# Reordering ScalarE around the query projections, the stores around the norms, and moving paired gate products to VectorE in a two-layer encoder kernel

## The chip, the cores and the metric

The kernel runs on one core of a Trainium2 chip. The metric is the device time of one execution in microseconds (us); the time shown for the kernel before is the median of three runs.

## The reference

256 tokens of width 1024 pass two layers. Each layer has an attention mixer and an expert mixer, each followed by a layer norm:

```python
for i in range(2):
    m = _mla_mixer(...) if i == 0 else _dsa_mixer(...)
    x = _layernorm(DN_ALPHA * x + m, ln_gain[i, 0], ln_bias[i, 0])
    f = _peer(x, peer_w_q[i], peer_sub_keys[i], peer_w_down[i], peer_w_up[i])
    x = _layernorm(DN_ALPHA * x + f, ln_gain[i, 1], ln_bias[i, 1])

def _peer(x, w_q, sub_keys, w_down, w_up):
    q = (xt @ w_q).reshape(T, 8, 2, 128)
    s1, s2 = scores of both halves of q against 128 sub-keys for each head
    v1, i1 = lax.top_k(s1, 16);  v2, i2 = lax.top_k(s2, 16)
    best, pos = lax.top_k(v1 + v2 over all pairs, 16)       # for each token and head
    gate = softmax(best)                                    # 128 experts for each token
    a = x . w_down[expert];  y = sum(gelu(a) * gate * w_up[expert])
```

The expert mixer has 128 x 128 = 16384 experts.

## The kernel before

**Numbers as pairs.** Every float32 weight and activation becomes two float16 parts: `hi`, a rounded copy that ScalarE casts (line 89), and `lo`, the remainder that VectorE computes with a running sum (line 98). One product is three float16 matmuls (hi.hi, hi.lo, lo.hi), issued by `mm` (line 340). Activations are `xh` and `xl`.

**The weight stream.** All weights pass in one fixed order through the class `Stream`, in blocks of 128 x 1024. A block is loaded by SyncE's queue (line 133) into one of six `raw` buffers, cast to `hi`, reduced to `lo`, used by TensorE, and dropped; there are six `hi` and six `lo` buffers. `get` hands out the next block and first splits blocks up to three further on (`AHEAD`) and issues loads up to five beyond those. Four blocks of the query weights are loaded ahead into the arena (line 141). With `ws.share = POOLED`, every fourth block is split in another way: ScalarE scales it in place (line 164) and casts it (166), GpSimd subtracts (168), and ScalarE later sums the result (177). In the stretches with much VectorE work this takes load off VectorE.

**Order.** A scheduler that simulates the program decides the order of instructions on each engine. `tc.issue_after` forces one instruction behind another of the same engine. `chains` holds such forced orders by engine: while `chains["dve"]` is open, all that is issued through `dve(...)` keeps the program's order; `act(...)` and `pe(...)` do the same where their chain is open.

**The norms (`finish`).** The last four weight blocks of a mixer are multiplied first for token tile 0 and then for tile 1, so that norm 0 runs on VectorE and ScalarE while TensorE does tile 1. `queue` keeps the order written out by hand on each engine. `Turned` transposes a normed tile on TensorE and splits it; the first four blocks of what follows (values of the second attention, or queries of the experts) are then multiplied part by part. A part is named by two letters, activation first: `lh` is `xl` with the block's `hi`. `ws.open` queues a block's cast, `ws.close` its `lo`. The normed tiles go to DRAM (`keep`, lines 515 and 529) and come back much later.

**The queries (`peer`).** The first 512 query columns come out of `finish` in two PSUM banks; `unscale` copies them out (line 372), `turn` transposes them (1080, 1081). `queries(n)` then projects two blocks and copies the result into `qT`; `scores(g4)` multiplies four of them with the keys and copies the scores (1103) to SBUF. The choosing of experts (`choose`, lines 1106 to 1170) is VectorE work that `spend` deals out in the program's order between the blocks.

**The down projection and the gates.** 128 blocks of `w_down` follow, two for a round of the loop. Once the choice is made, each round also calls `prepare` for one or two groups of four tokens: VectorE compares (line 1241, `hot`), GpSimd multiplies half of the comparison by the gates (1243), ScalarE multiplies the other way (1247). In the next round `place` lets TensorE combine them (`G`) and ScalarE and VectorE copy the result to the arena (1260, 1262). `hot` and `gate` have two buffers each. 60 of the 64 groups come two in a round. Then follow 128 blocks of `w_up` and the next norm.

Of the kernel before, what the change touches and what calls it, by code (L numbers as in the profile page):

```python
# [15 lines left out]
ALU = mybir.AluOpType  # L16
AX = mybir.AxisListType

P = 128
# [81 lines left out]
class Stream:  # L101
# [94 lines left out]
    def open(self, queue):  # L196

        i = self.n_split
        assert i == self.n_taken
        self._high(i, lambda emit: queue("act", emit))  # L200
        self.n_split += 1
        self.n_taken += 1
        return i
# [38 lines left out]
def tile_trunk(ctx: ExitStack, tc: tile.TileContext, ins, out: bass.AP, short, shared):  # L242
    nc = tc.nc
    half = F16 if short else F32R
    unit, ranks, total_unit = (UNIT, RANKS, SUM) if short else (1.0, 1.0, 1.0)
# [31 lines left out]
    keep = [dram.tile([P, D], F32, tag=f"x{t}", name=f"x{t}") for t in range(2)]  # L277
# [3 lines left out]
    gate16 = const.tile([P, T], F16, tag="gate16", name="gate16")  # L281
# [18 lines left out]
    ws = Stream(nc, raws, rings, half, split, spare16)  # L300
# [17 lines left out]
    chains = {}  # L318
# [17 lines left out]
    def act(emit):  # L336
        return link("act", emit)
# [33 lines left out]
    def unscale(o, p, unit):  # L371
        return nc.scalar.mul(o, p, 1.0 / unit) if short else nc.scalar.copy(o, p)
# [99 lines left out]
    def finish(y4, lhs_of, n, g, b, x, spare, lead=None):  # L472

        blks = [ws.get(ahead=0) for _ in range(STAGGER)]
        queue = queue_of()
        last = None
        norms = []  # L480
        for t in range(2):
            with ExitStack() as order:
                if last is not None:
                    order.enter_context(tc.issue_after(last.ins))
                for i, blk in enumerate(blks):
                    k = n - STAGGER + i
                    last = rows(y4, lhs_of(k), blk, k == 0, k == n - 1, (t,))
            if lead is not None:
                norms.append(Norm(queue, x[t], y4[t], g, b, spare[t], spare[2 + t], spare[4]))
        if lead is None:  # L490
            if short:
                judge()

            def close():
                queue = queue_of()
                for t in range(2):
                    norm = Norm(queue, x[t], y4[t], g, b, spare[t], spare[2 + t], spare[4], shared["st"][t])
                    norm.sums()
                    norm.square()
                    norm.centre()  # L500
                    norm.scale()
                    norm.result()
                for t in range(2):
                    for h, q in enumerate((nc.sync, nc.scalar)):
                        s = slice(h * 512, (h + 1) * 512)
                        q.dma_start(out[t * P : (t + 1) * P, s], spare[t][:, s])

            return close
        n0, n1 = norms
        n0.sums()  # L510
        n0.square()
        n0.centre()
        n0.scale()
        n0.result()
        nc.sync.dma_start(keep[0], spare[0])
        queue("pe", lambda: last)
        x0, x1 = Turned(queue, 0, spare[0]), Turned(queue, 1, spare[1])
        blk = [ws.open(queue) for _ in range(3)]
        n1.sums()
        x0.high(0, 2)  # L520
        x0.high(1, 4)
        n1.square()
        x0.low(0)
        n1.centre()
        blk.append(ws.open(queue))
        n1.scale()
        x0.low(1)
        n1.result()
        nc.sync.dma_start(keep[1], spare[1])
        unit = lead(queue)  # L530

        def do(t, part, *ks):
            for k in ks:
                unit(t, part, k, ws.ready[blk[k]])

        do(0, "hh", 0, 1, 2)
        do(0, "lh", 0, 1, 2)
        do(0, "hh", 3)
        do(0, "lh", 3)
        x1.high(0, 2)  # L540
        x1.high(1, 4)
        do(1, "hh", 0, 1, 2, 3)
        ws.close(blk[0], queue)
        ws.close(blk[1], queue)
        x1.low(0)
        do(0, "hl", 0, 1)
        do(1, "lh", 0, 1)
        do(1, "hl", 0, 1)
        ws.close(blk[2], queue)
        x1.low(1)  # L550
        do(0, "hl", 2)
        do(1, "hl", 2)
        do(1, "lh", 2)
        ws.close(blk[3], queue)
        do(0, "hl", 3)
        do(1, "hl", 3)
        do(1, "lh", 3)

    def weigh_up(part, lo, hi):

# [489 lines left out]
    def peer(li):  # L1050
# [3 lines left out]
        qT, keys = ar.take(16, T), ar.take(16, NKEYS)  # L1054
        s = [ar.take(16, NKEYS) for _ in range(2)]
# [12 lines left out]
        scr = ar.ring(2, NKEYS)  # L1068
        qrow = [arena[:, middle - (2 - t) * 512 : middle - (1 - t) * 512] for t in range(2)]
        tail = s[0].rearrange("p a b -> p (a b)")  # L1070
        nc.sync.dma_start(keys, ins["keys"][li].rearrange("n p k -> p n k"))

        for t, q in enumerate(begun.pop("q")):
            unscale(qrow[t], q, unit)

        def turn():
            for t in range(2):
                p = ps(f"qwT{t}")
                for n in range(4):
                    nc.tensor.transpose(p[:, n * P : (n + 1) * P], qrow[t][:, n * P : (n + 1) * P], ident)  # L1080
                nc.scalar.copy(qT[:, 0:4, t * P : (t + 1) * P], p.rearrange("p (n t) -> p n t", t=P))

        def queries(n):
            p = ps(f"pq{n}")
            pv = p.rearrange("p (j t) -> p j t", t=T)
            first = proj(pv[:, 0, :], ws.get())
            if n == FIRST:
                with tc.issue_after(first.ins):
                    turn()
            else:  # L1090
                spend(PACE)
            proj(pv[:, 1, :], ws.get())
            if n > FIRST:
                spend(PACE)
            unscale(qT[:, n : n + 2, :], pv, unit)

        def scores(g4):
            for t in range(2):
                p = py((2 * g4 + t) % 4, f"ps{g4}{t}")
                for j in range(4):  # L1100
                    n = 4 * g4 + j
                    mm(p[:, j * P : (j + 1) * P], qT[:, n, t * P : (t + 1) * P], keys[:, n, :], True, True)
                nc.scalar.copy(s[t][:, 4 * g4 : 4 * g4 + 4, :], p.rearrange("p (j k) -> p j k", k=P))

        def top16(vals, ids, src, buf):
            dve(lambda: nc.vector.max(vals[:, 0:8], src))
# [115 lines left out]

        chains["dve"] = None
        ws.dve = dve
        queries(4)
        ws.share = POOLED
        scores(0)
        queries(6)
        scores(1)
        for g4 in range(2, 4):  # L1230
            queries(4 * g4)
            queries(4 * g4 + 2)
            scores(g4)

        onehot = {}

        def prepare(g4):
            hot = ohp.tile([P, 2, P, 4], F16, tag="V", name="hot")
            gate = ohp.tile([P, 2, 4, P], F16, tag="U", name="gate")
            four = slice(4 * g4, 4 * g4 + 4)  # L1240
            nc.vector.tensor_tensor(hot, iota4[:, None].to_broadcast([P, 2, P, 4]),  # L1241
                                    place16[:, :, None, four].to_broadcast([P, 2, P, 4]), op=ALU.is_equal)
            nc.gpsimd.tensor_tensor(gate[:, 0], hot[:, 1].rearrange("p c j -> p j c"),  # L1243
                                    gate16[:, four, None].to_broadcast([P, 4, P]), op=ALU.mult)
            for j in range(4):
                t = 4 * g4 + j
                nc.scalar.mul(gate[:, 1, j, :], hot[:, 1, :, j], rest[:, t : t + 1])  # L1247
            onehot[g4] = hot, gate
# [18 lines left out]
        for b0 in range(0, NKEYS, 2):  # L1267
            p = ps(f"d{b0}")
            pv = p.rearrange("p (j t) -> p j t", t=T)
            chosen = ready  # L1270
            for j in range(2):
                proj(pv[:, j, :], ws.get())
                ready = ready or spend(PACE)
            if b0 == 0:
                chains["pe"] = None
            t0 = 4 * groups
            if t0 < T:
                nc.scalar.activation(A[:, b0 : b0 + 2, t0:], pv[:, :, t0:], AF.Gelu, scale=1.0 / unit)
            if t0 > 0:
                nc.scalar.activation(pv[:, :, :t0], pv[:, :, :t0], AF.Gelu, scale=1.0 / unit)  # L1280
                nc.vector.tensor_tensor(A[:, b0 : b0 + 2, :t0], A[:, b0 : b0 + 2, :t0], pv[:, :, :t0], op=ALU.mult)
            while groups < prepared:
                place(groups, b0 + 2)
                groups += 1
            if chosen:
                left = max(1, (NKEYS - 4 - b0) // 2)
                want = min(64 - groups, -(-(64 - groups) // left))
                assert want <= 2
                for _ in range(want):
                    prepare(prepared)  # L1290
                    prepared += 1
        assert groups == 64, groups
        chains.pop("pe")
# [188 lines left out]
```

## Time and profile before

| | |
|---|---|
| median of 3 runs | 1723.12 us (1722.04 to 1723.86) |
| the profiled execution's own time | 1721.89 us |
| span in its profile | 1720.0 us |
| TensorE busy | 1700.1 us (99%) |
| VectorE / ScalarE / GpSimd busy | 1346.4 / 1096.4 / 393.6 us |
| moved from DRAM | 329.16 MB |

The rows are read so: a group of instructions has its line in the kernel, engine, operation, output and inputs; then shape, count, total busy time and mean duration; behind the bar's second part stands how long the engine had been idle in front of them and what ended that. A row of the timeline has start and length in us. DVE is VectorE, ACT is ScalarE, POOL is GpSimd, PE is TensorE, SP is the queue of DMAs.

### The profile page before, as it was taken

The page shows a single profiled execution, that of the slowest core. Times are in us where ns is not written, and L with a number is a line of the kernel's source. Part 1 is how long each engine was busy: PE and PEld are TensorE (multiplying, and loading weights), DVE is VectorE, ACT ScalarE, POOL GpSimd, SP SyncE. Part 2 cuts the span into 40 slices and gives each one's busy share as a digit, 9 for nine tenths or more (in the row PEclk, how much of TensorE's full clock was granted, in tenths as well). Part 3 has the DMA queues.
Part 4 walks back from the last instruction along what each step waited for, and adds up shares of the span by engine and source line. Part 5 has one row for each costly group of instructions (what it writes and reads, how often), then busy time and mean ns, then how long its engine had stood idle before and what let it go on. Part 6 is the DMA issues. An engine that isn't in the chain of part 4 may idle for free.

```text
span 1720.0 us, 33157 instructions
## 1 busy us (share of the span) xinstructions
PE 1700.1 (99%) x12495; PEld 1191.9 (69%) x12495; DVE 1346.4 (78%) x3032; ACT 1096.4 (64%) x1910; POOL 393.6 (23%) x257
## 2 busy tenths in 40 slices
PE   9999999999999999999999999999999999999998
PEld 7678888899984444444577698888999954444443
DVE  7679999989996566666688798999899966666665
ACT  7666656888875555555477656567888755554553
POOL 2011244555530000000022012454555400000000
PEclk9999999999999999999999999999999999999999
DMA  9454556655567666666565555566555576666662
GB/s 350 138 177 169 198 190 204 204 172 172 173 194 244 200 207 201 203 205 201 185 229 186 183 184 177 193 205 223 173 173 173 173 248 204 206 201 204 203 202 77
DMA packets 93483, 335.61 MB, mean 195 GB/s; under 512 B 10368, under 2 KB 11392, under 8 KB 93312
## 3 DMA queue, kind: packets, MB, share of 16 engines
q1 hardware_dynamic: 93024, 332.87, 58.6%
q8 instruction: 100, 1.64, 0.4%
q14 instruction: 71, 0.58, 0.1%
q10 hardware_dynamic: 288, 0.52, 0.1%
HBM read 329.16 MB, written 4.19 MB: 194 GB/s over the span
## 4 chain that ended last, share of the span: by engine, by line
PE 87%; DVE 5%; ACT 3%; issue 2%; DMA 1%; POOL 1%; DVEq 0%; POOLq 0%; ACTq 0%
PE y L340 40%; PE d L340 36%; PE G L340 3%; PE pq L340 2%; DVE lo L98 2%; ACT hi L89 1%; PE qw L340 1%; PE h L340 1%; PE ps L340 1%; PE qi L340 1%; PE o L340 0%; PE v L340 0%; DVE arena L997 0%; PE qn L340 0%; DMA raw<-in_down 0%
## 5 line engine op out<-in xcount | busy, mean ns | idle before, releaser
L98 DVE SCALAR_TENSOR_TENSOR lo<-raw,hi 128x1024 f16<-128x1024 f32 (+1 forms) x571 | 776.6, 1363 | 237.4 <-ACT hi L89 233.6
L89 ACT ACTIVATE hi<-raw 128x1024 f16<-128x1024 f32 (+1 forms) x571 | 594.6, 1049 | 292.2 <-PE y L340 183.4
L340 PE MATMUL d<-xh,lo 128*128 128x256 f16 x2048 | 558.3, 273 | 1.7 <-DVE lo L98 1.5
L340 PE MATMUL d<-xh,hi 128*128 128x256 f16 x2048 | 558.2, 273 | 0.0
L340 PE MATMUL d<-xl,hi 128*128 128x256 f16 x2048 | 558.2, 273 | 0.0
L340 PEld LDWEIGHTS <-hi 128*128 128x128 f16 x5016 | 488.1, 98 | 57.9 <-issue 1.3
L340 PEld LDWEIGHTS <-xh 128*128 128x128 f16 x2320 | 226.4, 98 | 270.8 <-ACT xh L89 2.4
L340 PE MATMUL y<-lo,xh 128*128 128x512 f16 x1088 | 326.3, 379 | 0.0
L340 PE MATMUL y<-hi,xh 128*128 128x512 f16 x1088 | 326.0, 379 | 0.0
L340 PE MATMUL y<-hi,xl 128*128 128x512 f16 x1088 | 325.6, 379 | 0.0
L340 PEld LDWEIGHTS <-lo 128*128 128x128 f16 x2508 | 245.5, 98 | 32.7 <-DVE lo L98 3.7
L1243 POOL TENSOR_TENSOR gate<-hot,gate 128x512 f16<-128x512 f16 x128 | 219.7, 1736 | 186.8 <-DVE hot L1241 186.8
L340 PEld LDWEIGHTS <-xl 128*128 128x128 f16 x1160 | 113.3, 98 | 138.1 <-DVE xl L98 2.5
L1247 ACT ACTIVATE gate<-hot,rest 128x128 f16<-128x128 f16 x512 | 165.8, 410 | 8.1 <-DVE hot L1241 8.1
L89 ACT ACTIVATE xh<-arena 128x512 f16<-128x512 f32 x132 | 82.5, 628 | 132.5 <-PE y L340 132.2
L98 DVE SCALAR_TENSOR_TENSOR xl<-arena,xh 128x512 f16<-128x512 f32 x134 | 91.7, 687 | 60.0 <-ACT xh L89 59.9
L168 POOL TENSOR_TENSOR lo<-raw,hi 128x1024 f16<-128x1024 f32 x26 | 58.0, 2232 | 194.8 <-ACT hi L166 155.8
L438 POOL TENSOR_TENSOR st<-st,mhalf 128x1 f32<-128x1 f32 x6 | 3.3, 554 | 414.2 <-DVE st L436 414.2
L164 ACT ACTIVATE raw<-raw 128x1024 f32<-128x1024 f32 x26 | 27.5, 1056 | 101.2 <-DMA raw<-in_down 81.3
L1165 POOL TENSOR_TENSOR arena<-arena 128x800 f32<-128x800 f16 x32 | 72.4, 2262 | 70.4 <-DVE arena L1162 62.2
L1241 DVE TENSOR_TENSOR hot<-iota,place 128x1024 f16<-128x1024 f16 x128 | 82.8, 689 | 7.0 <-PE G L340 4.6
L580 POOL TENSOR_SCALAR fit<-fit 128x2 f32<-128x2 f32 x1 | 0.2, 227 | 316.2 <-DVE junk L562 316.2
(209 smaller groups left out, 1574.6 us busy)
## 6 DMA issues: line engine op xcount, KB each, us to landing
raw<-in_down SPq DMA_DIRECT2D x256, 512.0 KB, 3.3
raw<-in_up SPq DMA_DIRECT2D x256, 512.0 KB, 4.3
raw<-in_peer_q SPq DMA_DIRECT2D x24, 512.0 KB, 4.5
raw<-in_dsa_qk SPq DMA_DIRECT2D x16, 512.0 KB, 4.8
raw<-in_mla_w_o SPq DMA_DIRECT2D x8, 512.0 KB, 5.8
arena<-in_peer_q SPq DMA_DIRECT2D x8, 512.0 KB, 6.0
raw<-in_dsa_v SPq DMA_DIRECT2D x8, 512.0 KB, 4.4
raw<-in_dsa_w_o SPq DMA_DIRECT2D x8, 512.0 KB, 3.9
```

What stands on the lines that cost most here:

```text
L89: return nc.scalar.copy(o, src) if unit == 1.0 else nc.scalar.mul(o, src, unit)
L98: return nc.vector.scalar_tensor_tensor(o, src, unit, hi, op0=ALU.mult, op1=ALU.subtract, accum_out=total)
L164: self.act(lambda: nc.scalar.mul(raw, raw, unit))
L168: nc.gpsimd.tensor_tensor(lo, raw, hi if short else hi.bitcast(F32), op=ALU.subtract)
L340: return pe(lambda: nc.tensor.matmul(o, l, r, start=start, stop=stop, skip_group_check=True))
L438: nc.gpsimd.tensor_tensor(st[:, 5:6], st[:, 4:5], mhalf, op=ALU.pow)
L580: nc.gpsimd.tensor_scalar(fit[:, 0:2], fit[:, 0:2], MOST * SMALL, None, op0=ALU.is_lt)
L1165: nc.gpsimd.tensor_tensor(o.rearrange("p k c -> p c k"), same, cell[t][:, h, :, None].to_broadcast([P, CELLS, TOPK]), op=ALU.mult)
L1241: nc.vector.tensor_tensor(hot, iota4[:, None].to_broadcast([P, 2, P, 4]), place16[:, :, None, four].to_broadcast([P, 2, P, 4]), op=ALU.is_ ...
L1243: nc.gpsimd.tensor_tensor(gate[:, 0], hot[:, 1].rearrange("p c j -> p j c"), gate16[:, four, None].to_broadcast([P, 4, P]), op=ALU.mult)
L1247: nc.scalar.mul(gate[:, 1, j, :], hot[:, 1, :, j], rest[:, t : t + 1])
```

## The change

Four parts:

1. In `finish`, the casts of the next two blocks are queued ahead of norm 0's work on ScalarE, and the `lo` of the first ahead of norm 0's work on VectorE. A part `hl` of block 0 moves forward between the `lh` parts. The store of tile 1 is issued behind the last weight load of this place.
2. In `peer`, `chains["act"]` is opened, so that ScalarE follows the program from here to the end of the queries; the keys' load is put behind a weight load.
3. The queries take blocks without splitting further ones (`get(0)`); `ws.fill` splits the next ones behind the copies of the scores.
4. `prepare` gives the gates' product (line 1243) to VectorE in rounds with two groups, to GpSimd in rounds with one.

```diff
@@ finish
+        blk = [ws.open(queue) for _ in range(2)]
+        ws.close(blk[0], queue)
         n0.sums()
         n0.square()
...
         x0, x1 = Turned(queue, 0, spare[0]), Turned(queue, 1, spare[1])
-        blk = [ws.open(queue) for _ in range(3)]
+        blk.append(ws.open(queue))
...
         n1.result()
-        nc.sync.dma_start(keep[1], spare[1])
...
         do(0, "hh", 0, 1, 2)
-        do(0, "lh", 0, 1, 2)
+        do(0, "lh", 0, 1)
+        do(0, "hl", 0)
+        do(0, "lh", 2)
...
         do(1, "hh", 0, 1, 2, 3)
-        ws.close(blk[0], queue)
         ws.close(blk[1], queue)
         x1.low(0)
-        do(0, "hl", 0, 1)
+        do(0, "hl", 1)
...
+        with tc.issue_after(ws.last):
+            nc.sync.dma_start(keep[1], spare[1])
@@ peer
-        nc.sync.dma_start(keys, ins["keys"][li].rearrange("n p k -> p n k"))
+        chains["act"] = None
+        ws.act = act
+        ws.fill(ws.n_taken + 1)
+        with tc.issue_after(ws.last):
+            nc.sync.dma_start(keys, ins["keys"][li].rearrange("n p k -> p n k"))
         for t, q in enumerate(begun.pop("q")):
-            unscale(qrow[t], q, unit)
+            act(lambda: unscale(qrow[t], q, unit))
+        ws.fill(ws.n_taken + 3)
...  (the copies in turn, queries and scores go through act(...) likewise)
         def queries(n):
-            first = proj(pv[:, 0, :], ws.get())
+            i = ws.n_taken
+            first = proj(pv[:, 0, :], ws.get(0))
...
-            proj(pv[:, 1, :], ws.get())
+            proj(pv[:, 1, :], ws.get(0))
...
+            return i + 5
...
-        queries(4)
+        upto = queries(4)
         ws.share = POOLED
         scores(0)
-        queries(6)
+        ws.fill(upto)
+        upto = queries(6)
         scores(1)
+        ws.fill(upto)
         for g4 in range(2, 4):
-            queries(4 * g4)
-            queries(4 * g4 + 2)
+            ws.fill(queries(4 * g4))
+            upto = queries(4 * g4 + 2)
             scores(g4)
+            ws.fill(upto)
+        chains.pop("act")
...
-        def prepare(g4):
+        def prepare(g4, engine):
...
-            nc.gpsimd.tensor_tensor(gate[:, 0], hot[:, 1].rearrange("p c j -> p j c"),
-                                    gate16[:, four, None].to_broadcast([P, 4, P]), op=ALU.mult)
+            engine.tensor_tensor(gate[:, 0], hot[:, 1].rearrange("p c j -> p j c"),
+                                 gate16[:, four, None].to_broadcast([P, 4, P]), op=ALU.mult)
...
-                    prepare(prepared)
+                    prepare(prepared, nc.gpsimd if want == 1 else nc.vector)
```

More of the change, by code (lines that the diff above doesn't have):

```diff
@@ L198, in open @@
         i = self.n_split
-        assert i == self.n_taken
         self._high(i, lambda emit: queue("act", emit))
@@ L1080, in turn @@
                     nc.tensor.transpose(p[:, n * P : (n + 1) * P], qrow[t][:, n * P : (n + 1) * P], ident)
-                nc.scalar.copy(qT[:, 0:4, t * P : (t + 1) * P], p.rearrange("p (n t) -> p n t", t=P))
+                act(lambda: nc.scalar.copy(qT[:, 0:4, t * P : (t + 1) * P], p.rearrange("p (n t) -> p n t", t=P)))
         def queries(n):
@@ L1091, in queries @@
                 spend(PACE)
-            proj(pv[:, 1, :], ws.get())
+            proj(pv[:, 1, :], ws.get(0))
             if n > FIRST:
                 spend(PACE)
-            unscale(qT[:, n : n + 2, :], pv, unit)
+            act(lambda: unscale(qT[:, n : n + 2, :], pv, unit))
+            return i + 5
         def scores(g4):
@@ L1102, in scores @@
                     mm(p[:, j * P : (j + 1) * P], qT[:, n, t * P : (t + 1) * P], keys[:, n, :], True, True)
-                nc.scalar.copy(s[t][:, 4 * g4 : 4 * g4 + 4, :], p.rearrange("p (j k) -> p j k", k=P))
+                act(lambda: nc.scalar.copy(s[t][:, 4 * g4 : 4 * g4 + 4, :], p.rearrange("p (j k) -> p j k", k=P)))
         def top16(vals, ids, src, buf):
```

## The prediction

> **What bounds the kernel now.** I read the page first, then TensorE's waits, then the chain of waits, then the timeline at the three places that the change touches.
>
> ```profile
> span 1720.0 us, 33157 instructions
> PE 1700.1 (99%) x12495; PEld 1191.9 (69%) x12495; DVE 1346.4 (78%) x3032; ACT 1096.4 (64%) x1910; POOL 393.6 (23%) x257
> ```
>
> TensorE is busy in 99% of the span. The change removes no matmul, so all that it can win is idle time of TensorE, 19.9 us in the whole span, start and end included. TensorE's waits, in total, times, longest:
>
> ```profile
> PE G L340 <- POOL gate L1243: 1.8, 4, 0.5
> PE d L340 <- DVE lo L98: 1.5, 2, 1.0
> PE ps L340 <- ACT arena L372: 1.4, 1, 1.4
> PE qw L340 <- DVE xl L98: 1.3, 2, 0.8
> ...
> PE qwT L1080 <- ACT arena L372: 0.7, 1, 0.7
> ```
>
> Four rows belong to the change: G 1.8, ps 1.4, qw 1.3, qwT 0.7, together 5.2 us in eight waits. A wait costs more than its idle time shows, because the end of a matmul is drawn late:
>
> ```profile
> L340 PE MATMUL d<-xh,hi 128*128 128x256 f16 x2048 | 558.2, 273 | 0.0
> 328.10 5.24 PE d L340 x48
> ```
>
> A matmul lasts 273 ns in the record, but 48 take 5.24 us, 109 ns each. So each wait hides a further 0.16 us, and eight are worth 5.2 + 1.3 = 6.5 us. That is the ceiling of this change at its own places, 0.4% of the run. By the spread of the runs before (1722.04 to 1723.86), about 0.2%, 3.4 us, can be told from no change.
>
> **The change part by part.**
>
> *Norms.* Casting two blocks ahead of norm 0 (two ScalarE casts of about 1 us, one `lo` of 1.2 us on VectorE) falls into idle time at the first norm:
>
> ```profile
> 83.05 1.15 ACT L426 ACTIVATE arena<-arena,st 128x1024 f32<-128x1024 f32 x1 [4.98 <-DVE st L421]
> 81.46 0.69 DVE L418 SCALAR_TENSOR_TENSOR arena<-arena,y 128x512 f32<-128x512 f32 x1 [1.93 <-PE y L340]
> 90.08 0.68 DVE L98 SCALAR_TENSOR_TENSOR xl<-xt,xh 128x512 f16<-128x512 f32 x1
> 90.83 0.60 PE L340 MATMUL qw<-hi,xl 128*128 128x512 f16 x2 [0.55 <-DVE xl L98]
> 957.04 1.06 ACT L164 ACTIVATE raw<-raw 128x1024 f32<-128x1024 f32 x1 [5.53 <-DMA raw<-in_peer_q]
> 958.01 1.13 ACT L426 ACTIVATE arena<-arena,st 128x1024 f32<-128x1024 f32 x1
> 956.88 0.21 DVE L421 TENSOR_SCALAR st<-st 128x1 f32<-128x1 f32 x1
> ```
>
> ScalarE waits 4.98 us and VectorE 1.93 us for TensorE there, so the early work costs nothing while raw data and ring slots are in place; without that cover, norm 0 would move by up to 1.2 us. TensorE then reaches `lh` of block 2 before `xl` is there (0.55 us). The moved `hl` of block 0 is two matmuls of 0.216 us that need no new `xl`: 0.43 us of this wait is filled. At the norm of the second attention the same wait is about 0.76 us (1.3 less 0.55). There ScalarE scaled a block of the queries (957.04, waiting for its DMA) in front of norm 0's square, which VectorE had made ready at 957.1; it started at 958.01. With the forced order that scaling belongs behind the scores, so norm 0 comes 0.9 us sooner and the wait goes whole, 0.92 us with its hidden part. Sum: -0.43 - 0.92 = -1.35 us. The norm before the second attention's values has no row among the waits: 0.
>
> *Store and keys.* SP's queue is in order:
>
> ```profile
> 92.63 1.71 SPq L529 DMA_DIRECT2D x<-arena  x1
> 94.45 12.73 SPq L133 DMA_DIRECT2D raw<-in_peer_q  x6
> 101.65 1.06 ACT L164 ACTIVATE raw<-raw 128x1024 f32<-128x1024 f32 x1 [3.05 <-DMA raw<-in_peer_q]
> 103.56 1.06 ACT L372 ACTIVATE arena<-qw 128x512 f32<-128x512 f32 x2
> ```
>
> The store of tile 1 waits for the norm's result, and six loads wait behind it until 94.45. ScalarE then stands 3.05 us for that data, and the copy of the first queries (103.56), ready about 101, comes late: TensorE's wait for it (qwT) is 0.7 us. Loads in front, and the copies in front of further casts, take this away: -0.89 us. The store is read hundreds of us later; the keys are needed by the first scores, which come behind the copies of 103.56, some 10 us after the store's turn: 0 for both. That slack is the keys' cover; without it the scores would wait.
>
> *Queries.* The wait at ps has the same kind of cause:
>
> ```profile
> 137.87 1.06 ACT L164 ACTIVATE raw<-raw 128x1024 f32<-128x1024 f32 x1 [5.71 <-DMA raw<-in_down]
> 139.78 0.58 ACT L372 ACTIVATE arena<-pq 128x512 f32<-128x512 f32 x1
> 118.83 1.07 ACT L1103 COPY arena<-ps 128x512 f32<-128x512 f32 x2
> 119.00 2.13 POOL L168 TENSOR_TENSOR lo<-raw,hi 128x1024 f16<-128x1024 f32 x1 [10.19 <-ACT hi L166]
> 126.48 1.06 PE L340 MATMUL ps<-arena 128*128 128x128 f32 x8
> ```
>
> The last query copy (139.78) stood behind a scaling that waited 5.71 us for a down block. In the new order that block's work follows the copy: -1.4 - 0.16 = -1.58 us. But the order also takes something. In the first expert mixer the block that goes through GpSimd is the first one split behind each of three scores. From the end of a query block ScalarE now copies (0.6), waits for scores (1.1), copies (1.1), scales and casts (2.0), then GpSimd takes 2.13: 6.9 us. TensorE meanwhile has 0.9 us of scores and 48 matmuls, 5.2 us, and needs the `lo` 0.2 us later: 6.3 us. Up to 0.6 us late, three times: between 0 and 1.8, I take 1.0. In the second mixer the GpSimd block is the second of its pair and has a block's 24 matmuls, 2.6 us, more: 0.3 for what I don't see (bounds 0 and 1.6, one more ps wait). VectorE's choosing starts behind the same `lo` as before, so nothing comes from there.
>
> *Gates.* At the start of each gate stage GpSimd is late for four G's: -1.8 - 4 x 0.16 = -2.44 us. The price is VectorE's time in the 29 rounds that follow, in each mixer:
>
> ```profile
> L1241 DVE TENSOR_TENSOR hot<-iota,place 128x1024 f16<-128x1024 f16 x128 | 82.8, 689 | 7.0 <-PE G L340 4.6
> 327.76 1.29 DVE L1241 TENSOR_TENSOR hot<-iota,place 128x1024 f16<-128x1024 f16 x2
> 328.97 2.08 DVE L98 SCALAR_TENSOR_TENSOR lo<-raw,hi 128x1024 f16<-128x1024 f32 x1
> 338.76 1.23 DVE L98 SCALAR_TENSOR_TENSOR lo<-raw,hi 128x1024 f16<-128x1024 f32 x1 [0.37 <-ACT hi L89]
> 328.53 3.43 POOL L1243 TENSOR_TENSOR gate<-hot,gate 128x512 f16<-128x512 f16 x2 [2.43 <-DVE hot L1241]
> ```
>
> Four rounds as windows (us; PE, PEld, DVE, ACT, POOL busy):
>
> ```profile
> 327.04:333.18 6.14, 6.14 (x67) 5.61 (x66) 5.37 (x10) 5.47 (x14) 3.43 (x2) 1.00 0.56 191
> 376.11:382.24 6.13, 6.13 (x66) 5.60 (x65) 5.60 (x10) 5.39 (x14) 3.44 (x2) 1.00 0.52 169
> 425.18:431.31 6.13, 6.13 (x67) 5.60 (x64) 5.89 (x10) 5.28 (x14) 3.44 (x2) 1.00 0.50 172
> 492.64:498.78 6.14, 6.14 (x67) 5.61 (x66) 6.12 (x10) 5.12 (x14) 3.44 (x2) 1.00 0.54 175
> ```
>
> TensorE needs 6.13 us for a round; VectorE 5.37 early and 6.12 late, since its copies of G grow. One `lo` of each round takes 2.08 us, not 1.23, beside GpSimd: without GpSimd's products VectorE gets 0.85 us back. A gate product has 512 elements. No row shows it on VectorE. The nearest is `hot`, the same operation kind, 1024 float16 elements, 0.60 us from start to start (1.29 - 0.69). `lo`, also 1024 elements, takes 1.23 (1.15 from start to start): `hot` does two elements in the time of one, so 512 at one each cost what `hot` costs, 0.60. Lower bound 0.35 (two each again); upper bound 1.15, the price of 1024 single ones. I take 0.60, and 1.20 for the pair: VectorE's round grows by 0.35, to 5.72 early and 6.47 late. From the middle of the stage it exceeds 6.13 by 0 to 0.34, over some 15 rounds 2.5 us in all. TensorE feels that once the gates come later than its 5.24 us of `d`: two compares and two gates end 2.4 us into a round, 3.5 with a `lo` between them, so 1.7 to 2.8 us are covered. I take +0.8 us for each mixer, +1.6. `lo` late by 2.5 us is no harm: casts run as far ahead as the ring of six blocks lets them. ScalarE's part is unchanged; GpSimd is free.
>
> [...] ScalarE reads the same tile with the same step, and its rows show no surcharge beside a contiguous operand of the same count, both with a per-token operand:
>
> ```profile
> L1247 ACT ACTIVATE gate<-hot,rest 128x128 f16<-128x128 f16 x512 | 165.8, 410 | 8.1 <-DVE hot L1241 8.1
> L680 ACT ACTIVATE arena<-arena,m 128x128 f32<-128x128 f32 x16 | 6.6, 411 | 5.1 <-DVE m L673 5.1
> ```
>
> 410 against 411 ns: so I stay near the lower price.
>
> *Sum.* -1.35 - 0.89 - 1.58 + 1.0 + 0.3 - 2.44 + 1.6 = -3.36 us. The profiled execution took 1721.89 us for a span of 1720.0; it becomes 1718.5. The median of the runs lies 1.2 us above it, so I predict 1719.7 us.
>
> **Rivals.**
>
> *VectorE becomes the bound of the gate stage* (the other side). It decides at about 0.62 us for a gate: then the mean round, 5.74 - 0.85 + 1.25, is 6.13. If each gate waits for its own `hot` to finish (0.69 in place of 0.60, some 0.12 with the start), the pair costs 1.44 and the overrun is about 6.8 us for each mixer, less 2.7 covered: +8.2 in place of +1.6, 1726 us. If a gate needs 1.15 us, every round overruns, on the mean by 1.0 us: 30 less 2.7 us for each mixer, +55, about 1773 us. For it: 0.62 is a hair above 0.60. Against it: hots start in pairs, so the scheduler can put both in front; and the ScalarE rows.
>
> *The queries give it back.* ScalarE in program order lets the three GpSimd blocks come late by more than 0.6 us, or ps wait in both mixers: +2.5 us on the sum, 1722 us. For it: the 6.9 us against 6.3 above. Against: in the old order no wait of TensorE is longer than 1.4 us outside the start, whatever stood in front on ScalarE.
>
> *All waits go and nothing new comes.* -6.3 us, and the two waits d for `lo` (1.5 idle, 1.8 in full) shift too: 1715 us.
>
> **How the numbers follow.** The forecast's case (1716 to 1722) 0.45, give-back 0.18, all gone 0.15, overrun by waiting for `hot` 0.12, by slow reads 0.10. The range 1715 to 1727 takes in all but slow reads and half of the ends. 0.2% faster is below 1719.7, the forecast itself: half of its case and all of the fifth: about 0.40. Slower is above 1726.5: slow reads and much of the other overrun, 0.18. The rest, 0.42, is no change that can be told.
>
> **What would show it.** Right: no wait of G for gates, of qwT or of ps for line 372; the qw waits under 0.4 us; line 1243 on DVE near 0.69 us, `lo` at 1.23 throughout the gate stage, VectorE's last full rounds without idle time; GpSimd idle there. Wrong: line 1243 above 0.8 us on DVE; rounds longer than 6.13 us; pq or ps waiting for POOL or ACT at 110 to 140 us.

## The result, and the profile after

The changed kernel takes 1732.25 us (median of 5 runs, 1730.43 to 1732.95) against 1722.04 us (1721.59 to 1723.86, 5 runs) of the kernel before beside it: a ratio of 1.0054, interval 1.0042 to 1.0065. It is 0.5% slower. The forecast was 1719.7 us, a little faster, with a range of 1715 to 1727.

The head of the page after:

```profile
span 1730.5 us, 33129 instructions
PE 1704.9 (99%) x12495; PEld 1192.1 (69%) x12495; DVE 1365.1 (79%) x3156; ACT 1102.5 (64%) x1910; POOL 184.7 (11%) x133
```

The same 12495 matmuls, in a span 10.5 us longer. TensorE's waits after (in total, times, longest):

```profile
PE d L339 <- DVE lo L98: 6.0, 8, 1.6
PE idle L1359 <- DVE iotac L292: 2.5, 1, 2.5
PE pq L339 <- POOL lo L168: 1.8, 1, 1.8
PE d L339 <- POOL lo L168: 1.8, 1, 1.8
PE G L339 <- DVE gate L1256: 1.3, 4, 0.3
...
PE d L339 <- ACT hi L166: 0.8, 1, 0.8
PE ps L339 <- ACT arena L371: 0.7, 1, 0.7
PE pq L339 <- DVE lo L98: 0.7, 1, 0.7
```

The waits at qw and qwT have left the list, G's is smaller, ps's is halved. New are waits of the queries (pq) for `lo`, and waits of pq and d for GpSimd; the waits of the down projection (d) for `lo` have grown from 1.5 us to 6.0. In all, the rows of d and pq that are shown hold 11.1 us of idle time, where before there were 1.5.

Idle time shows a wait too short (a matmul of `d` lasts 273 ns in the record, and the next starts 0.11 us after its start), so I also took, for every two matmuls that follow each other, the time from start to start beyond the median of the same shape; I call it TensorE's excess. Its sum is 17.8 us before and 28.3 after, and the difference, 10.5 us, is that of the spans. By stage (stages in us of the span; only matmuls that are more than 25 ns late, 18.5 and 28.9 us in all):

| stage | before | after |
|---|---|---|
| 88-111, norm and first queries | 1.86 | 0.68 |
| 111-141, queries and scores, first mixer | 1.76 | 3.45 |
| 141-216, down projection beside the choosing | 0.00 | 7.56 |
| 216-324, up to the gates | 3.42 | 1.27 |
| 324-520, gate stage | 0.00 | 0.24 |
| 955-975, second norm | 1.65 | 0.68 |
| 975-1110, queries, scores, choosing, second mixer | 0.00 | 5.71 |
| 1110-1392, the rest of it, gates | 1.95 | 1.42 |
| all other | 7.86 | 7.86 |

So the loss arises where the queries are, and behind them, in both mixers: 9.2 us more between 111 and 216, of which the next stage gets 2.2 back, and 5.7 us more in the second mixer. About 1.7 of the 7.56 us are not waiting: from 151.6 to 155.3 us the granted clock is 0.54, where it is 1.00 behind, and 16 matmuls follow each other at 0.21 us instead of 0.11. This is not the loss itself: it is 1.7 of 10.5 us, and the kernel with the queries' part alone, below, loses as much at a mean granted clock of 0.999 over its profiled run, that of the kernel before (the changed kernel's is 0.998). That the waits in front (0.77 and 1.81 us, up to 151.6) bring the clock down isn't shown; after a wait of 1.81 us at 136.4 it stays at 1.00.

The chain of waits between 105 and 325 us (start, duration, what), before and then after:

```profile
138.84 1.04 ACT hi L89
140.41 1.16 PE ps L340 x8
141.57 2.84 PE d L340 x26
144.41 0.89 PE ps L340 x8
145.30 67.81 PE d L340 x621
```

```profile
134.07 1.14 ACT spare L177 x2
135.22 0.96 ACT hi L89
136.20 1.26 DVE lo L98 x2
...
145.32 0.71 ACT raw L164
146.04 5.42 issue
151.45 1.23 DVE lo L98 x2
...
204.79 1.29 DVE lo L98 x2
206.13 20.82 PE d L339 x189
```

Before, the chain runs on TensorE for 68 us without a break from 145.30. After, it leaves ScalarE at 136.2 and stays on VectorE until 206.13, but for one scaling on ScalarE at 145.32 and the 5.42 us behind it, in which VectorE does nothing. VectorE has become the bound of this stage although no work was added to it there. The shares of the whole span can't show this: VectorE is at 79% of the span, and it binds in one stage. The same stage as windows (us; busy time and count of PE, PEld, DVE, ACT, POOL; clock, DMA share, GB/s), before and after:

```profile
100.00:216.00 116.00, 113.84 (x1037) 102.11 (x1036) 101.85 (x398) 75.11 (x100) 24.17 (x17) 1.00 0.54 181
```

```profile
100.00:216.00 116.00, 108.21 (x959) 94.67 (x957) 92.24 (x367) 75.03 (x97) 24.21 (x16) 0.99 0.49 162
```

VectorE does 9.6 us less in the same 116 us. What it waits for between 98 and 216 us, before and after:

```profile
DVE arena L1106 <- ACT arena L1103: 6.0, 1, 6.0
DVE lo L98 <- ACT hi L89: 3.6, 4, 1.1
DVE lo L98 <- issue: 0.2, 1, 0.2
```

```profile
DVE lo L98 <- ACT hi L89: 14.3, 4, 5.3
DVE lo L98 <- issue: 5.6, 2, 5.4
```

9.8 us of waiting became 19.9. Before, 6.0 of it was the wait for the first scores, and 3.6 were for casts. After, 14.3 are for ScalarE's casts by name; the profile names nothing for the 5.4 us up to 151.45, but ScalarE casts from 150.32, one block in about 1.04 us, and VectorE's `lo` starts just behind the end of the first of these casts. The timeline shows why the casts are late (start, duration; the idle time before it and what ended it in brackets; ScalarE's rows first, then what waits for them):

```profile
127.78 0.60 ACT L371 ACTIVATE arena<-pq 128x512 f32<-128x512 f32 x1 [4.38 <-PE pq L339]
131.06 1.07 ACT L1112 COPY arena<-ps 128x512 f32<-128x512 f32 x2 [2.69 <-PE ps L339]
132.02 1.07 ACT L164 ACTIVATE raw<-raw 128x1024 f32<-128x1024 f32 x1
133.12 1.04 ACT L166 CAST hi<-raw 128x1024 f16<-128x1024 f32 x1
...
135.12 1.04 ACT L89 ACTIVATE hi<-raw 128x1024 f16<-128x1024 f32 x1
136.20 1.25 DVE L98 SCALAR_TENSOR_TENSOR lo<-raw,hi 128x1024 f16<-128x1024 f32 x1 [2.69 <-ACT hi L89]
134.25 2.12 POOL L168 TENSOR_TENSOR lo<-raw,hi 128x1024 f16<-128x1024 f32 x1 [11.97 <-ACT hi L166]
136.42 0.28 PE L339 MATMUL pq<-xh,lo 128*128 128x256 f16 x1 [1.81 <-POOL lo L168]
```

ScalarE stands 4.38 us for the last query matmul and 2.69 us for the scores. The raw data of the two blocks that it works on next landed at 114.55 and 116.64 us, but they stand behind the copies in its fixed order, one scaled and the other cast only at 132.02 and 135.12. When the scores are copied, it has a scaling and the casts to do in a row; VectorE and GpSimd wait for them, and TensorE waits for GpSimd.

### The profile page after: what moved, and what is told of

It reads as the page before. It is cut to its first block, busy times and chain, and to the rows that moved or that the text cites. A ratio compares the mean times of both kernels' runs of the same rounds, so it can differ in the third digit from the quotient of the medians.

```text
span 1730.5 us, 33129 instructions
## 1 busy us (share of the span) xinstructions
PE 1704.9 (99%) x12495; PEld 1192.1 (69%) x12495; DVE 1365.1 (79%) x3156; ACT 1102.5 (64%) x1910; POOL 184.7 (11%) x133
## 4 chain that ended last, share of the span: by engine, by line
PE 81%; DVE 12%; issue 3%; ACT 3%; DMA 1%; POOL 1%; SPq 0%; DVEq 0%; POOLq 0%; ACTq 0%
PE y L339 40%; PE d L339 29%; DVE lo L98 5%; PE G L339 3%; PE pq L339 2%; DVE arena L1116 1%; DVE arena L1119 1%; ACT hi L89 1%; DVE arena L1118 1%; PE qw L339 1%; DVE arena L1117 1%; PE h L339 1%; DVE arena L1115 1%; PE v L339 1%; PE ps L339 0%
## 5 line engine op out<-in xcount | busy, mean ns | idle before, releaser
L98 DVE SCALAR_TENSOR_TENSOR lo<-raw,hi 128x1024 f16<-128x1024 f32 (+1 forms) x571 | 722.3, 1269 | 244.1 <-ACT hi L89 237.5
L1256 DVE TENSOR_TENSOR gate<-hot,gate 128x512 f16<-128x512 f16 x124 | 84.2, 683 | 0.0
L339 PE MATMUL G<-gate,hot 128*128 128x128 f16 x1024 | 68.6, 219 | 1.3 <-DVE gate L1256 1.3
L339 PEld LDWEIGHTS <-hot 128*128 128x128 f16 x1024 | 64.5, 113 | 3.1 <-issue 1.8
L1275 DVE SCALAR_TENSOR_TENSOR arena<-G,arena 128x256 f32<-128x256 f32 (+32 forms) x128 | 65.2, 536 | 0.0
```

The source lines that it names most:

```text
L98: return nc.vector.scalar_tensor_tensor(o, src, unit, hi, op0=ALU.mult, op1=ALU.subtract, accum_out=total)
L339: return pe(lambda: nc.tensor.matmul(o, l, r, start=start, stop=stop, skip_group_check=True))
L1256: engine.tensor_tensor(gate[:, 0], hot[:, 1].rearrange("p c j -> p j c"), gate16[:, four, None].to_broadcast([P, 4, P]), op=ALU.mult)
L1275: nc.vector.scalar_tensor_tensor(A[:, :done, tsl], pv[:, :done, :], 1.0 / GSCALE, A[:, :done, tsl], op0=ALU.mult, op1=ALU.mult)
```

## The experiments

The expectations name theories by letters: A, late casts on ScalarE; in the form A1 the late place of the casts (`fill` behind the scores' copies), by which VectorE loses its choosing time; in the form A2 the fixed order on ScalarE. E: the place of the block that goes through GpSimd. F: the late casts delay TensorE whatever VectorE's own order is. B, C and D are explained where they first come. All ratios are against the kernel before on the same chip.

**Which part.** Four kernels hold parts of the change alone, on the kernel before: part 4 (`prepare(prepared, nc.gpsimd if want == 1 else nc.vector)`), part 1 (the new `finish`), both, and parts 2 and 3 (the new `peer` order, `get(0)` and `fill`).

> The kernel before with the fourth part alone (VectorE multiplies the paired gates). Theory A (the loss comes from the casts that stand behind the scores' copies): in the changed kernel the gate product took 0.68 us on VectorE and TensorE waited 1.3 us in all for gates, against 1.8 for GpSimd before; so 0 to 2.5 us less than before, 1720 to 1722 us, no wait for lo in the gate stage. Rival B (VectorE overloaded by the gates makes it late for all that follows): at least 5 us more than before.

> The kernel before with the first part alone (early casts, hl moved forward, store later). Theory A: TensorE's waits at the two norms in front of queries shrink by 1.35 us as in the changed kernel (two waits of 0.11 us are left of 0.55 and 0.76), and the six loads no longer stand behind the store, so the waits of qwT (0.7) and perhaps ps (1.4) shrink too: 1 to 3.5 us less than before, 1718.5 to 1721 us. Rival C (the early casts or the later store do harm that shows in the queries): equal or slower than before.

> The kernel before with the first and fourth parts, without the new order of the queries. Theory A: the sum of the two runs above, 1 to 5 us less than before, 1717 to 1721 us. Rivals B and C: 5 us more than before or worse.

> The kernel before with the second and third parts alone (ScalarE in the program's order at the queries, casts behind the scores' copies, keys' load later). Theory A: it carries the whole loss, 8 to 14 us more than before, 1730 to 1736 us, with VectorE idle for casts at 100 to 150 us and TensorE waiting for lo at 130 to 210 us. Rivals B and C: within 3 us of before.

Measured: gates 1721.46 us, ratio 0.9999 (0.9990 to 1.0008); norms 1720.00, 0.9987 (0.9978 to 0.9996); both 1720.59, 0.9989 (0.9980 to 0.9998); queries 1733.79, 1.0071 (1.0057 to 1.0084). The kernel before took 1721.91. So the queries' order alone costs 11.9 us, norms and gates together win 1.3, and the sum, +10.6, agrees with the change's +10.2: there is no sign that the parts act on each other. All four came as theory A expected; B and C fall. TensorE's excess between 111 and 216 us is 10.59 us in the queries' kernel and 11.01 in the changed one, 1.76 before.

**Which half of the queries' part.** First the fixed order without the late casts:

```diff
-            first = proj(pv[:, 0, :], ws.get(0))
+            first = proj(pv[:, 0, :], ws.get())
...
-        ws.fill(upto)
...
```

> The changed kernel with blocks again split three ahead by get(), and without the four fills behind the scores; ScalarE still follows the program. Theory A1 (the loss needs the casts to stand behind the copies; the forced order alone is harmless): casts are then in front of the copies that wait for TensorE, VectorE's idle time for casts at 100 to 216 us falls from 14 to under 6 us, and the time is at most 1723 us. Theory A2 (ScalarE in program order is enough to make VectorE late, wherever the splits stand): 1728 us or more.

Then the late casts without the fixed order:

```diff
-        chains["act"] = None
-        ws.act = act
...
-        chains.pop("act")
```

> The changed kernel without the forced order on ScalarE; the splits still stand behind the scores in the program, and VectorE's chain still has lo behind the choosing. Theory A1: the scheduler can put casts in front of waiting copies, but a lo still stands behind the choosing it was moved behind; between, 1721 to 1727 us. Theory A2: all of the loss goes, 1721 us or less. Rival D (the place of lo in VectorE's chain is the cause): all of the loss stays, 1730 us or more.

And the changed kernel with each `ws.fill(upto)` one line higher, in front of its `scores`:

> The changed kernel with each fill in front of the scores instead of behind them: casts no longer wait for the scores' matmuls and copies, 3 to 4 us sooner in each round, all else the same. Theory A1: VectorE's waits for casts (4.0, 2.7 us and so on) mostly go, 1721 to 1726 us. Theory D: within 2 us of the changed kernel.

Measured: 1723.01 us, ratio 1.0010 (1.0000 to 1.0020); 1720.15, 0.9989 (0.9979 to 0.9998); 1721.48, 1.0002 (0.9992 to 1.0011), where the kernel before took 1721.85. Against the kernel before, neither half costs much by itself, the first 0.2% at most, the second nothing. (These three kernels also hold the new norms and gates, which win 1.3 us. Counted from there, by the medians, the fixed order alone costs some 2.5 us, the free order nothing, the casts in front 0.9.) So it takes both: a ScalarE bound to its order, and casts that stand in that order behind copies which wait for TensorE. Moving the casts by one line takes the loss away.

The three expectations were met only in part. A2 asked for 1728 us or more with the order alone and is out. A1 asked for 1721 to 1727 us with the free order, and the 1720.15 is what A2 expected; D, which asked for 1730, is out. VectorE's waits for casts between 98 and 216 us were to fall under 6 us with the order alone and mostly to go with the casts in front; they are 9.5 and 12.2 us, where the changed kernel has 14.3 and the 5.4 without a name. TensorE's excess between 111 and 216 us fell to 3.90 and 2.79 all the same. The stage 100 to 216 us in the kernel with the casts in front, and then in the one with free order:

```profile
100.00:216.00 116.00, 113.87 (x1035) 101.56 (x1034) 99.42 (x396) 79.63 (x105) 23.61 (x17) 1.00 0.53 177
```

```profile
100.00:216.00 116.00, 116.00 (x1059) 104.38 (x1057) 102.42 (x401) 76.69 (x102) 26.25 (x18) 1.00 0.55 185
```

TensorE is back at 113.87 and at a full 116.00 us, VectorE at 99 and 102.

**Rival E: GpSimd's block.** Two of TensorE's new waits name GpSimd. Here the pooled block is the second one split behind each score in the first mixer, so that it is needed later:

```diff
-            if pooled or self.share and (i - 1) % self.share == 0:
+            if pooled or self.share and (i - 1 - self.phase) % self.share == 0:
...
+        ws.share, ws.phase = POOLED, 1 - li
```

> The changed kernel with GpSimd's block one later in the first expert mixer, so that it is the second of its pair and TensorE needs it 2.6 us later. Rival E (the loss in the first mixer is GpSimd's late lo: TensorE waited 1.8 + 1.8 us for it and 1.2 for its cast): 4 to 6 us less than the changed kernel, 1726 to 1728 us. Theory A1: VectorE is late anyhow, and then TensorE waits for VectorE's lo instead: less than 2.5 us less, 1730 to 1732 us.

Measured: 1734.00 us, 1.0071 (1.0054 to 1.0088): no gain where E expected 4 to 6 us, and above the 1730 to 1732 of A1 too. The waits changed their name:

```profile
PE d L339 <- DVE lo L98: 9.6, 13, 1.6
PE d L339 <- POOL lo L168: 1.9, 1, 1.9
```

One wait for GpSimd (1.8) went, and d now waits 9.6 us for VectorE's `lo` in place of 6.0. E falls: GpSimd's block passes on the delay and doesn't cause it.

**Is it VectorE's order?** A1 says that VectorE stands in its written order behind a `lo` that can't start. Here its `lo`s are outside that order while the queries run, so that it may choose meanwhile; the second line added stands behind the last scores:

```diff
-        ws.dve = dve
+        ws.dve = lambda emit: emit()
         upto = queries(4)
...
+        ws.dve = dve
```

> The changed kernel with lo taken out of VectorE's forced order during the queries (the choosing keeps its own), ScalarE unchanged. Theory A1 says that late casts hurt because VectorE stands still at a lo whose cast is late, with choosing queued behind it: then VectorE can choose meanwhile, its waits for casts at 98 to 216 us (14.3 and 5.6) fall below 8 in all, and the time is 1722 to 1728 us. Rival F (TensorE is late because the casts themselves come too late for it, the choosing doesn't matter): within 2 us of the changed kernel, 1730 us or more.

Measured: 1730.47 us, 1.0050 (1.0036 to 1.0065), as F expected; A1 expected 1722 to 1728. VectorE did go ahead, and then ran out of work:

```profile
DVE lo L98 <- issue: 12.1, 2, 11.9
DVE lo L98 <- ACT hi L89: 4.2, 3, 2.3
DVE arena L1115 <- ACT arena L1112: 3.5, 1, 3.5
```

```profile
100.00:216.00 116.00, 107.93 (x971) 95.12 (x970) 92.60 (x370) 74.17 (x99) 22.14 (x16) 1.00 0.48 161
```

It waits as long in sum, 19.8 us, now 11.9 of it in one piece up to 151.8, and it is as little busy (92.60). So in the first mixer it is not VectorE's order that loses the time but the casts' (F): until they come there is no work to be had, in whichever order. This corrects the theory's second half. Two things limit it. In the second mixer's stage TensorE's excess falls to 2.74 us from 5.71, so there VectorE's order had a share. And ScalarE's order did not stay quite the same: a scaling that waits 5.84 us for its load now stands in front of the last query copy (145.24, before 141.66), so part of the 11.9 us comes from there.

**Does each mixer pay for itself?** The casts in front of the scores in the second mixer alone (`if li: ws.fill(upto)` in front):

> The changed kernel with the casts put in front of the scores' copies in the second expert mixer alone; the first is as changed. By A1 (casts that stand behind copies which wait for TensorE, and VectorE idle for them) each mixer pays by itself, the first what its stages lost beyond before (about 7.3 us: 1.6 + 7.5 in the stages 111 to 216, less 1.9 at 216 to 300), the second about 4.3 us: the median is about 1728, VectorE's waits for `hi` stay near 14 us in the first mixer and fall to about 3 in the second. If the loss sits in one mixer alone, or comes from something else that both share, it is 1722 or 1732.

Measured: 1728.87 us, 1.0043 (1.0029 to 1.0057), beside 1721.26 for the kernel before; 1728 was expected. TensorE's excess between 975 and 1110 us goes from 5.71 to 0.00, of which 1.9 come back in the next stage (3.28 from 1.42), and in the first mixer it stays (11.32 between 111 and 216). So each mixer pays for itself. But VectorE's waits for `hi` in the second mixer (975 to 1130) fell only from 12.5 to 10.6 us, where 3 were expected. Their sum is thus no measure of the loss: 10.6 us of them cost TensorE at most the 3.28. What makes one wait cost more than another was not tested.

**Towards a better kernel.** Casts in front of the scores, with the pooled block second; then the same with one gate of each pair on GpSimd:

```diff
-                for _ in range(want):
-                    prepare(prepared, nc.gpsimd if want == 1 else nc.vector)
+                for n in range(want):
+                    prepare(prepared, nc.gpsimd if n == want - 1 else nc.vector)
```

> The kernel with casts ahead of the scores (1721.5), and GpSimd's block one later in the first mixer. There TensorE still waited 1.8 us for GpSimd's lo at the third of its blocks. If that wait counts once VectorE is in time, it goes: 1719 to 1720.5 us. If another wait takes its place: 1721 to 1722.

> The kernel above with one gate of each pair on VectorE and the other on GpSimd. In the changed kernel TensorE waited 1.3 us (2.0 with the hidden part) for gates in the second round of each mixer, because VectorE did three lo before them; and the last rounds overran by 0.25 us. With one gate each both go, VectorE's rounds end no later than before the change: 1.5 to 2.2 us less than the kernel above, 1717 to 1719 us. Rival: GpSimd's gate, 1.4 us or more, holds up a lo again and is late for the same G: no gain.

Measured: 1722.36 us, 1.0006 (0.9997 to 1.0015), and 1725.64, 1.0023 (1.0015 to 1.0032). The first is no gain, just above both of its expectations. The second missed its 1717 to 1719 by 7 us. The gates of this second kernel by engine (busy in all, mean ns of one):

```profile
L1256 DVE TENSOR_TENSOR gate<-hot,gate 128x512 f16<-128x512 f16 x62 | 92.6, 1493 | 0.0
L1256 POOL TENSOR_TENSOR gate<-hot,gate 128x512 f16<-128x512 f16 x66 | 128.7, 1951 | 283.2 <-DVE hot L1254 283.2
```

A gate takes VectorE 1.49 us while GpSimd makes its own, so one gate beside GpSimd is dearer than the two without it (1.29 us), and G waits ten times, 3.8 us in all.

Then the first mixer in free order with the casts behind the scores, the second in fixed order with the casts in front, once with one gate each and once with both gates on VectorE, as changed:

```diff
-        chains["act"] = None
+        if li:
+            chains["act"] = None
...
+        if li:
+            ws.fill(upto)
         scores(0)
         ws.fill(upto)
```

> As the kernel above, but the first mixer's queries in free order with splits behind the scores (that kernel had no wait of TensorE at 111 to 216 us there, 2.0 us at 975 to 1015), the second mixer's with casts ahead and forced order (0.0 there). If the stretches add up: 1717 to 1719 us, the same as the kernel above; if the free order leaves later waits, 1719 to 1721.

> The changed kernel, both gates of a pair on VectorE as changed, ScalarE in free order with the casts behind the scores in the first mixer, and in program order with the casts ahead of the scores in the second. A1: nothing of the loss is left, the norms' gain (-1.4) and the waits qwT and ps stay won, and G's waits for gates are gone or small: 1717 to 1719, below both kernels. Rival (the pair on VectorE still makes late `lo`s or G's in the second round, as 2 us of excess at the starts of the gate stages): 1719.5 to 1721, no better than the norms alone.

Measured: 1720.49 us, 0.9995 (0.9987 to 1.0004), and 1716.94 us (10 runs, 1715.80 to 1718.52), 0.9976 (0.9967 to 0.9986) against 1721.26. The first came within its second range (1719 to 1721), the last just under its 1717 to 1719. The last beats both kernels, by 0.24% against the one before. Its stage 100 to 216 us, and TensorE's first waits:

```profile
100.00:216.00 116.00, 116.00 (x1057) 104.28 (x1056) 103.00 (x401) 76.81 (x102) 26.22 (x18) 1.00 0.55 186
```

```profile
PE d L339 <- DVE lo L98: 1.6, 2, 0.9
PE G L339 <- DVE gate L1263: 1.3, 4, 0.4
```

TensorE's excess is 14.3 us (17.8 before, 28.3 after), 0.00 between 111 and 216. So nothing of the loss is left in the first mixer. Norms and gates win 1.3 us of the 4.3 by the run that holds them alone; there a wait for the last query copy (ps, 2.5 us) remained, which is not in this kernel. That 4.3 is near the 3.4 of the prediction is chance: this is another kernel, and its terms are other ones.

## Why the prediction was wrong, point by point

**The step that failed is the price of the queries, and in it one sentence: "VectorE's choosing starts behind the same `lo` as before, so nothing comes from there."** With it VectorE's share in the loss was put at nothing. The queries' loss was +1.0 +0.3 us beside -1.58 for ps and -0.89 for qwT; the part alone measured +11.9. The choosing did start as before (the first `max` at 112.28, 112.88 before). But between its pieces stand `lo`s, and their casts had moved behind copies that wait for TensorE. I followed one chain only, from ScalarE through GpSimd to TensorE's next need, and asked whether TensorE is late for that block. I didn't ask what VectorE, busy for 101.85 of 116 us, does while the casts are withheld. Of its 14 us of idle time in this window 9.8 were waits; the change made those 19.9, and the rest of the choosing and every `lo` behind it came late until 206 us. That the choosing stands behind a late `lo` is the smaller part: with the `lo`s outside its order VectorE chose ahead and most of the loss stayed (1730.47 us).

**The same chain was also too short by its own numbers.** I had 6.9 us from the end of a query block to GpSimd's `lo`, with 1.1 us of waiting for scores. The rows give 127.78 (copy) to 136.37 (end of `lo`), 8.6 us: TensorE puts query matmuls of the next block between the two groups of score matmuls, so ScalarE waits 2.69 us, not 1.1, before it copies. Against the 6.3 us of cover that is 2.3 us late; the trace has TensorE idle for 0.35 us for the `hi` and 1.81 for the `lo`, and 0.77 and 1.81 at the next score. "Up to 0.6 us late, three times" was about four times too small, twice. The prediction's own sign of being wrong, pq waiting for POOL at 110 to 140 us, is the wait at 136.42.

**The rival "The queries give it back" named this place** and priced it at +2.5 us. Its argument against was that before the change no wait of TensorE was longer than 1.4 us "whatever stood in front on ScalarE". That was evidence from a free order, in which the scheduler may put a cast in front of a copy that isn't ready. It says nothing of a fixed one, as the kernel in free order shows: same late casts, no loss.

**ps: -1.58** was half right: 0.7 of 1.4 us is left. It is another wait: the one behind a late load is gone, and a new one, of the scores at 121.56, stands behind a scaling and two casts on ScalarE (117.92 to 120.9), which the new order puts in front of that query copy. **qwT: -0.89** is right, the wait is gone, also in the kernel with the norms' part alone. **Norms: -1.35**; the two norm stages lost 3.51 us before and 1.36 after together with qwT, 2.15 us less against the 2.24 predicted, and the kernel with the norms' part alone ran 1.9 us faster than before.

**Gates: -2.44 + 1.6.** The price of a gate on VectorE was right:

```profile
L1256 DVE TENSOR_TENSOR gate<-hot,gate 128x512 f16<-128x512 f16 x124 | 84.2, 683 | 0.0
```

```profile
425.00:431.13 6.13, 6.13 (x66) 5.60 (x65) 6.06 (x12) 5.29 (x14) 0.00 (x0) 1.00 0.56 170
```

The first row is the group of the gates (busy in all, mean ns of one), the second a round from the middle of the stage as a window. In the first round, two gates in a row:

```profile
313.17 1.29 DVE L1256 TENSOR_TENSOR gate<-hot,gate 128x512 f16<-128x512 f16 x2
...
317.62 1.29 DVE L1254 TENSOR_TENSOR hot<-iota,place 128x1024 f16<-128x1024 f16 x2
318.82 1.22 DVE L98 SCALAR_TENSOR_TENSOR lo<-raw,hi 128x1024 f16<-128x1024 f32 x1
...
319.97 0.69 DVE L1256 TENSOR_TENSOR gate<-hot,gate 128x512 f16<-128x512 f16 x1
```

Two gates in 1.29 us are 0.60 from start to start, as assumed, and not the 1.15 of the upper bound, though `hot` is read at every fourth float16; the round is still TensorE's 6.13. The overrun was mis-sized, 0.24 us of excess in each gate stage where I had 0.8. The gain was mis-sized too: G still waits four times, 1.3 us, now for VectorE: in the second round of the first mixer the `hot`s start only at 317.62, behind `lo`s, another `lo` stands between them and the gate of 319.97, and TensorE's G at 320.71 waits 0.28 us for it.

As a whole the part, alone, wins 0.45 us, where 0.84 was forecast; its interval (0.9990 to 1.0008) takes in no change at all.

What stays open: how much of the loss passes through the raw buffers (a late `lo` keeps a buffer, so the next load and cast come late). One such turn stands in the trace: the `lo` of 140.53 ends at 141.7, a load is issued at 141.77 and lands at 145.23, and ScalarE's scaling, which had waited 3.06 us, starts at 145.31. The profile names VectorE's choosing for that wait; the landing fits better. This one held up little, since the scores that ScalarE copies next were done only at 145.37. With the `lo`s outside VectorE's order the wait for a load of 5.84 us does stand in front of a copy that was due. How many us of the loss come this way no run tells; a kernel with more raw buffers wasn't tried.

## What to carry to other kernels

When an engine is bound to the order of the program, work that others wait for belongs in front of work that waits for others: here the casts put one line behind the copies out of the accumulators cost 10 us against the kernel before, and one line in front of them nothing that can be told from it. For every instruction moved behind a waiting one, go through each engine that consumes it, not only the one that sets the end, and compare the new idle time with the slack of that engine in that window, not in the whole span. That no wait was seen under a free schedule is no argument for a fixed one.

## What the runs showed of the hardware that was not expected

Where a `lo` or a gate on VectorE met a gate on GpSimd, the later of the two ended about as if it had begun when the earlier was done. In the kernel with one gate each, a gate of 512 elements takes VectorE 1493 ns in the mean of 62, against 683 in the changed kernel, and the three that begin at 435.24, 441.56 and 447.92 us, 0.98 to 0.99 us after GpSimd's gate, end about 0.55 us behind it. In the kernel before, 64 `lo`s begin while GpSimd makes a gate; they end 1.08 to 1.09 us behind it and take 2.08 us, against 1.23. The other way round it is the same: the GpSimd gates that begin during such a `lo` end 0.90 to 0.92 us behind it and take 2.02 to 2.05 us, where one that meets neither `lo` nor `hot` takes 1.05 (at 504.08 us in the changed kernel). Moving one of two such products to GpSimd therefore made VectorE slower, not faster: its 62 gates take 92.6 us, the changed kernel's 124 take 84.2.

The gate reads `hot` at every fourth float16, and for one element it costs VectorE about what `lo` costs: 0.60 us from start to start for the gate's 512 elements (1.17 ns for one) and 1.15 us for the 1024 of `lo` (1.12 ns). For one element that is twice the price of `hot`, which writes 1024 in 0.60.
